# LayerNorm's factor rows, SiLU results and gated branch in PSUM instead of SBUF, and all low weights of that stage on GpSimd

## The chip, the cores and the metric

The kernel runs on one core of one Trainium2 chip. The metric is the device time of one execution in microseconds; smaller is better. The engines are TensorE (PE), VectorE (DVE), ScalarE (ACT), GpSimd (POOL) and the DMA queue of SyncE (SP). SBUF is the working memory, PSUM the eight banks that TensorE writes its products to.

## The reference, cut to what matters

Two layers on 512 tokens of width 1024, all in fp32. The change lies in the end of the first layer, between the convolution and the output projection.

```
u = a * sigmoid(b)                         # a, b, z = three parts of h @ w_in, 2048 channels each
c = depthwise causal convolution(u, 31 taps) + dw_b
mu, var = mean and variance of c over the 2048 channels of a token
cn = (c - mu) * rsqrt(var + EPS) * ln_g + ln_b
y  = silu(cn) * silu(z)
x  = x + y @ w_out                         # then layer 2: retention, and a last RMSNorm
```

## The kernel before, in words

Activations are held with channels in the partitions: the 2048 inner channels are 16 tiles of [128 channels, 512 tokens], one PSUM bank or 2 KB per partition each. Products in fp32 precision are made of three fp32r products: each operand is split into a high part (a rounded copy, by ScalarE) and a low part (the rest, a subtraction), and high x high, high x low and low x high are summed in PSUM. The same is done to the weights, which come as pairs of units of [128, 1024]: `whi(n)` is ScalarE's rounding of unit n (L181), `wlo(n, eng)` the subtraction by VectorE or GpSimd (L186). Of the raw weights two pairs fit into SBUF, of the high parts two pairs, of the low parts three.

The stage in question is LayerNorm and the output projection of layer 1 (L820 to L909). TensorE first sums over channels, VectorE makes the mean's rest `delta` and the factor `r` from [128, 4] values in 14 tiny operations (`rsqrt`, L249 to L261), and TensorE spreads each of the two over all partitions as a [128, 512] row in PSUM (`bcast_mm`, L267): `MUF` holds the mean, `RLp` the factor. ScalarE copies them to SBUF as `MU1` (L831) and `RL` (L894). While these small steps run, TensorE works off two gate units that were held back for it (`hold`, units 46 and 47).

Then, tile by tile (j = 0 to 15), `ln_a(j)` subtracts `MU1` (GpSimd, L859, five tiles ahead), `ln_b(j)` multiplies by the factor (VectorE, L863) and applies SiLU with gain and bias (ScalarE, L864), two tiles ahead; L884 multiplies by the gate `sz[j]` (VectorE), L886 rounds to the high part (ScalarE), L899 subtracts for the low part (VectorE), and twelve products of TensorE (L907 to L909, four output tiles of three) add the tile into four PSUM banks `acc4`. All of it stands in SBUF, except the rows `MUF` and `RLp` and the banks of `acc4`. Of the low weights, units 48, 50, 52, 54, 56 and 57 are GpSimd's and units 49, 51, 53 and 55 VectorE's.

In this stage every engine takes its instructions strictly in the order of the code. Behind it (L916 on) a scheduler orders them; the rotary tables (L935 to L967) are some 60 operations of VectorE that may begin behind the last `ln_b`, and the other half of the output projection (units 56 to 63, `x1_tile`) runs on TensorE meanwhile.

PSUM's eight banks are three pools: `MM` (5), `ACC` (2) and `ST` (1).

Of the kernel before, what the change touches and what calls it, by code (L numbers as in the profile page):

```python
# [20 lines left out]
S = 512            # tokens  # L21
NT = S // P        # token tiles
KD = 8             # 128-channel tiles of the model width
KI = 16            # 128-channel tiles of the inner width
W = 31             # taps
# [3 lines left out]
NU = 128           # weight units of [128, 1024]  # L29
PRODS = 3          # products that wait for GpSimd  # L30
ACCS = 2           # pairs of tiles with a sum of GpSimd
STEPS = 4          # at most so many taps of a pair of tiles are added by transfers
PAIRS = (2, 3, 4, 5)   # pairs of tiles with such taps
URING = 10         # tiles of the convolution's input
SPLIT = 12         # from this tile on VectorE and GpSimd have sums of their own (about M0)
APART = (1,) + tuple(range(SPLIT, KI))  # tiles with two sums
POOL_CAP = 16      # at most so many taps of a tile are summed by ScalarE and GpSimd
LEAD = 8           # taps that the last tile but one is ahead of the last
RATE = 1.6         # a product and its addition, as far as the choice of the next tile goes
MUP = 4            # so many of the first tiles TensorE sums for M0  # L40
HOLD = 2           # units that fill the gaps about the LayerNorm
GAP = 0.6          # products between two of its sums, so that TensorE's clock stays up
RESTS = 3          # sums of the last squares that are kept apart so
QLATE = 0.7        # margin for the end of the last transfer of squares
LNW = 2.8          # from the sums to the LayerNorm's factor
AHEAD = 5          # tiles that are centred ahead
TAILW = 10         # products that keep the clock up at the end
DMA_LAG = 1.55     # from the issue of a transfer to its start
# [6 lines left out]
def f12(v):  # L55
    """The nearest value with 12 significant bits."""
    m, e = np.frexp(v)
    return float(np.ldexp(np.round(m * 4096.0), int(e)) / 4096.0)
# [13 lines left out]
class Clock:  # L72
    """Estimated times (us) of engines that take instructions strictly in the order in which they are traced."""
# [13 lines left out]
    def land(self, cost, issued, key=None):  # L87
        """The end of a transfer."""
        return self.run(DMA_, cost, None, key, at=issued + DMA_LAG) + 0.1


@with_exitstack
def trunk(ctx: ExitStack, tc: tile.TileContext, xT, pos, wpack, conv_par, norms, freq, decay, out):
# [34 lines left out]
    def keep_warm(n):  # L128
        """Products of zeros: the tensor engine's clock drops to half when it idles."""
        o = ACC()  # L130
        for _ in range(n):
            nc.tensor.matmul(o, wz[:, 0:P], wz, start=True, stop=True)
# [56 lines left out]
    def neg_hi(p):  # L189
        """The high parts of a pair, negated, in the place of the low parts."""  # L190
        new_lo(p)
        it.run(ACT_, 1.8, lambda: nc.scalar.activation(los[p], raws[p], AF.Copy, scale=-1.0), f"wneg{p}")  # L192
# [5 lines left out]
    def dma_lo(p):  # L198
        """The transfer adds the weights to their negated high parts."""
# [18 lines left out]
    def split(src, eng=None, new=None):  # L218
        """src (fp32 in SBUF) as the exact sum of two fp32r tiles."""
# [5 lines left out]
    def mm3(o, a, b, first, last):  # L225
        """o += a.T @ b for split a and b."""
# [4 lines left out]
    def cm_proj(n, xs, k0=0, o=None, kt=KD, total=KD):  # L231
        """Channel-major projection of one unit (8 k-tiles x 128 columns)."""
# [8 lines left out]
    def rsqrt(v, scale=None, new=None):  # L241
        """v ** -0.5, or (v * scale + EPS) ** -0.5: a guess from the exponent's bits, a step of second order with
        constants that suit the guess's error, a step of third order."""
# [11 lines left out]
        # y is -guess / RSQRT_B; e = v guess ** 2; the result is guess (15 - 10 e + 3 e ** 2) / 8  # L255
# [8 lines left out]
    def bcast_mm(r4, o):  # L264
        """Per-token values [128 tokens, 4] as rows: [128, 512], the same in every partition."""
# [10 lines left out]
    def token_sums(tiles, o=None, first=True, last=True):  # L276
        """Sums over channels (partitions of all tiles), token-major [128, 4]."""
# [57 lines left out]
    # The taps of a tile: ScalarE multiplies and GpSimd adds the first ones, VectorE does the rest, on two tiles in  # L335
    # turn. How many are the first ones is set by how far GpSimd has come when VectorE gets to the tile. Some of the
    # products, of two tiles at once, are added by a transfer. The last tiles have a sum of VectorE, from the last tap
    # down, and one of GpSimd, from the first tap up.
    low = [0] * KI             # taps below are ScalarE's and GpSimd's
    high = [W] * KI            # in the last tiles: taps from here on are VectorE's  # L340
    acc_sb = [None] * KI       # GpSimd's sum
    acc_at = [0.0] * KI        # when it is there
    acc_ps = [None] * KI       # VectorE's sum
    begun = [0]                # tiles that VectorE has begun
    active = []
    latest = [None]            # the tile of VectorE's last instruction
    sums2 = {}                 # the places of GpSimd's sums, for two tiles each
    left2 = {}                 # how many of the two are not yet taken up
    freed = [0.0] * ACCS       # [n]: when the place of pair n is free
    steps = [0] * (KI // 2)    # taps of a pair of tiles that transfers add  # L350
    adds2 = deque()            # products of pairs that are yet to be added
    p2_free = [0.0]            # when their place is free
    adds = deque()             # products that GpSimd is yet to add
    stats = {"mu": 0, "d": 0, "pe": deque(), "sq": deque()}
    add_end = [0.0] * PRODS    # [n]: when the slot of product n is free
# [8 lines left out]
    def first_tap(j):  # L364
        """Tap 0 and the bias."""
# [12 lines left out]
    def release(j):  # L378
        """VectorE has taken up GpSimd's sum of tile j."""
# [4 lines left out]
    def room(j):  # L384
        """Whether tile j has a place for GpSimd's sum."""
        return j // 2 in sums2 or sum(n > 0 for n in left2.values()) < ACCS

    def pair_of(n):
        """The tiles of pair n that the next transfer can add to."""
# [67 lines left out]
    def ready(j):  # L457
        """When VectorE's next instruction of tile j can start."""
# [51 lines left out]
    def settled(j):  # L510
        """Whether the next product can be added to GpSimd's sum of tile j soon."""
        return acc_at[j] < it.now[POOL_] + 1.0 and all(a[0] != j // 2 for a in adds2)

    def pool_tile():
        """The tile that the next product is for."""
# [51 lines left out]
    # sums for LayerNorm: of the first tiles for M0, then of c - M0 (in the place of c) and of its square  # L567
# [696 lines left out]
```

## Time and profile before

| | |
|---|---|
| runs | 822.84, 824.01 and 825.59 us; median 824.01 us |
| profiled execution, first to last instruction | 821.5 us |
| TensorE busy in it | 790.3 us (96%) |
| VectorE, ScalarE, GpSimd busy | 606.6, 420.6 and 366.0 us |
| mean granted TensorE clock | 0.993 of 2.4 GHz |

For the profiled execution there is the span alone, 821.5 us; the runs, taken without the profiler, are 1.3 to 4.1 us longer than that, their median 2.5 us. The shares are means over stages with different limits; the stage of the change is some 60 us of the 821.5. Times within the trace count from the first instruction.

### The profile page before, as it was taken

What the parts mean: (1) busy time and instruction counts of PE and PEld (TensorE: products, weight loads), DVE (VectorE), ACT (ScalarE), POOL (GpSimd) and SP (SyncE); (2) the same over time, 40 slices, a digit from 0 to 9 for tenths busy, and PEclk for the clock granted to TensorE, in tenths of its full rate; (3) what the DMA queues carried; (4) which work ended last, traced back from release to release, by engine and by line L of the source; (5) the groups of instructions that cost most, each with busy time, mean ns of one, the idle gap of its engine ahead of it and who ended that gap; (6) DMA issues with size and microseconds to landing.
All of it is one profiled execution on the core that took longest, in us unless ns stands there. A gap on an engine that the chain in (4) does not pass through costs nothing.

```text
span 821.5 us, 9673 instructions
## 1 busy us (share of the span) xinstructions
PE 790.3 (96%) x3650; PEld 646.2 (79%) x3650; DVE 606.6 (74%) x852; ACT 420.6 (51%) x546; POOL 366.0 (45%) x287
## 2 busy tenths in 40 slices
PE   7889999999999998899999999999999999999996
PEld 3468878888888886578788888888888888888895
DVE  4788999999999979999955658566476557552324
ACT  4558888887987835444422433413423524341421
POOL 1439999999999975521311124223340122000300
PEclk9999999999999999999999999999999999999998
DMA  7497877887799742222232112213112212213103
GB/s 269 103 223 187 202 178 184 218 216 204 194 227 230 187 118 111 116 103 102 103 103 102 52 52 103 99 55 103 52 52 103 102 52 103 103 65 132 60 1 102
DMA packets 19901, 104.18 MB, mean 127 GB/s; under 512 B 2320, under 2 KB 5392, under 8 KB 8720
## 3 DMA queue, kind: packets, MB, share of 16 engines
q1 hardware_dynamic: 15392, 75.27, 25.7%
q0 software_dynamic: 4464, 28.31, 17.4%
q8 instruction: 28, 0.46, 0.2%
q14 instruction: 17, 0.14, 0.0%
HBM read 73.17 MB, written 2.10 MB: 92 GB/s over the span
## 4 chain that ended last, share of the span: by engine, by line
PE 78%; DVE 8%; POOL 4%; DMA 3%; ACT 3%; issue 3%; SPq 0%; DVEq 0%; POOLq 0%; ACTq 0%
PE mm L227 24%; PE mm L229 24%; PE mm L228 24%; DVE acc L497 3%; POOL accp L293 2%; DVE g L884 1%; DVE g L899 1%; DMA g<-xT 1%; DMA raw<-wpack 1%; POOL g L662 1%; ACT g L886 1%; DMA wlo<-raw 1%; PE dsum L282 1%; PE st L282 1%; DVE g L863 1%
## 5 line engine op out<-in xcount | busy, mean ns | idle before, releaser
L227 PE MATMUL mm<-g,whi 128*128 128x512 f32 (+1 forms) x832 | 320.2, 385 | 0.0
L229 PE MATMUL mm<-g,wlo 128*128 128x512 f32 (+1 forms) x832 | 316.9, 382 | 3.3 <-DMA wlo<-raw 3.3
L228 PE MATMUL mm<-g,whi 128*128 128x512 f32 (+1 forms) x832 | 317.4, 381 | 0.0
L497 DVE SCALAR_TENSOR_TENSOR acc<-u,cpar,acc 128x512 f32<-128x512 f32 x311 | 209.8, 746 | 0.5
L293 POOL TENSOR_TENSOR accp<-accp,prod 128x512 f32<-128x512 f32 x138 | 190.0, 1402 | 9.9 <-ACT prod L427 3.4
L229 PEld LDWEIGHTS mm<-g,wlo 128*128 128x128 f32 x832 | 156.5, 188 | 33.5 <-DMA wlo<-raw 3.7
L227 PEld LDWEIGHTS mm<-g,whi 128*128 128x128 f32 x832 | 156.5, 188 | 30.5 <-issue 1.2
L228 PEld LDWEIGHTS mm<-g,whi 128*128 128x128 f32 x832 | 156.5, 188 | 30.3 <-issue 1.2
L181 ACT CAST whi<-raw 128x1024 fp32r<-128x1024 f32 x80 | 80.5, 1048 | 101.3 <-PE mm L228 57.4
L186 DVE TENSOR_TENSOR wlo<-raw,whi 128x1024 fp32r<-128x1024 f32 x74 | 100.5, 1389 | 41.2 <-ACT whi L181 41.2
L293 POOL TENSOR_TENSOR g<-g,g 128x512 f32<-128x512 f32 x23 | 34.2, 1488 | 181.3 <-ACT g L289 172.7
L427 ACT ACTIVATE prod<-u,cpar 128x512 f32<-128x512 f32 x138 | 95.0, 717 | 25.7 <-POOL accp L293 25.2
L995 POOL TENSOR_TENSOR g<-g,g 128x512 f32<-128x512 f32 x8 | 10.3, 1293 | 140.0 <-DVE g L993 140.0
L222 DVE TENSOR_TENSOR g<-g,g 128x512 fp32r<-128x512 f32 x36 | 29.0, 820 | 35.7 <-ACT g L221 32.2
L221 ACT CAST g<-g 128x512 fp32r<-128x512 f32 x36 | 22.4, 621 | 60.0 <-POOL g L995 27.8
L228 PE MATMUL mm<-wlo,g 128*128 128x512 f32 x128 | 49.8, 389 | 0.0
L229 PE MATMUL mm<-whi,g 128*128 128x512 f32 x128 | 49.6, 389 | 0.0
L227 PE MATMUL mm<-whi,g 128*128 128x512 f32 x128 | 49.3, 389 | 0.0
L192 ACT ACTIVATE wlo<-raw 128x2048 fp32r<-128x2048 f32 x23 | 43.9, 1907 | 8.1 <-DMA raw<-wpack 8.1
L196 ACT CAST whi<-raw 128x2048 fp32r<-128x2048 f32 x23 | 43.7, 1898 | 0.0
L200 POOL DMA_DIRECT2D wlo<-raw x23 | 20.2, 877 | 38.1 <-ACT wlo L192 37.4
L1062 POOL TENSOR_TENSOR o<-o,g 128x512 f32<-128x512 f32 x16 | 27.5, 1749 | 18.2 <-DVE g L261 18.2
(193 smaller groups left out, 990.5 us busy)
## 6 DMA issues: line engine op xcount, KB each, us to landing
raw<-wpack SPq DMA_DIRECT2D x63, 1024.0 KB, 4.8
wlo<-raw POOLq DMA_DIRECT2D x23, 1024.0 KB, 7.2
g<-xT SPq DMA_DIRECT2D x16, 256.0 KB, 5.1
q<-q POOLq DMA_DIRECT2D x6, 512.0 KB, 7.5
out_dram<-xo SPq DMA_DIRECT2D x6, 256.0 KB, 2.3
dec<-decay SPq DMA_DIRECT2D x1, 1280.0 KB, 7.4
raw<-wpack SPq DMA_DIRECT2D x4, 256.0 KB, 5.9
accp<-prod POOLq DMA_DIRECT2D x2, 512.0 KB, 5.9
```

The lines of the kernel that those rows point to most:

```text
L181: it.run(ACT_, 0.95, lambda: nc.scalar.copy(his[p][:, i, :], raws[p][:, i, :]), f"whi{n}")
L186: it.run(e, c, lambda: eng.tensor_tensor(out=lo, in0=raws[n // 2][:, n % 2, :], in1=hi.bitcast(F32), op=ALU.subtract), f"wlo{n}", [f"whi{n}"])
L192: it.run(ACT_, 1.8, lambda: nc.scalar.activation(los[p], raws[p], AF.Copy, scale=-1.0), f"wneg{p}")
L196: it.run(ACT_, 1.8, lambda: nc.scalar.copy(his[p], raws[p]), f"whi{p}", deps)
L222: (eng or nc.vector).tensor_tensor(out=lo, in0=src, in1=hi.bitcast(F32), op=ALU.subtract)
L227: nc.tensor.matmul(o, a[0], b[0], start=first, stop=False)
L228: nc.tensor.matmul(o, a[0], b[1], start=False, stop=False)
L229: nc.tensor.matmul(o, a[1], b[0], start=False, stop=last)
L293: eng.tensor_tensor(out=a, in0=a, in1=b, op=ALU.add)
L427: at = it.run(ACT_, 0.61, lambda: nc.scalar.activation(p, u_sb[j][:, w:w + S], AF.Copy, scale=cpar[:, j, w:w + 1]), at=add_end[n_prod[0]])
L497: it.run(DVE_, cost, lambda: nc.vector.scalar_tensor_tensor(out=c_sb[j] if last else acc, in0=u_sb[j][:, w:w + S], scalar=cpar[:, j, w:w + 1],
L1062: nc.gpsimd.tensor_tensor(out=t, in0=t, in1=RO, op=ALU.mult)
```

## The change

The diff without its removed comments (line numbers of the code before are those of the kernel shown above):

```diff
@@ the bank that products of zeros go to, before the LayerNorm @@
-    idle = ACC()
+    idle = MM()
@@ LayerNorm's rows @@
     MUF = ACC()
     it.run(PE_, 0.86, lambda: bcast_mm(delta, MUF), "mu", at=t0 + 0.2)
     MU1 = G()
-    it.run(ACT_, 0.5, lambda: nc.scalar.copy(MU1, MUF), None, ["mu"])
     r = rsqrt(var)
-    wlo(49, nc.vector)
+    nc.vector.tensor_copy(MU1, MUF)
     work(t0 + LNW)
     RLp = ACC()
     it.run(PE_, 0.86, lambda: bcast_mm(r, RLp), "r", at=t0 + LNW)
-    RL = G()
@@ ln_a @@
-        nc.gpsimd.tensor_tensor(out=t, in0=t, in1=MU1, op=ALU.subtract)
+        if j < 2:
+            nc.vector.tensor_tensor(out=t, in0=t, in1=MUF, op=ALU.subtract)
+        else:
+            nc.gpsimd.tensor_tensor(out=t, in0=t, in1=MU1, op=ALU.subtract)
+    t_ps = {}
@@ ln_b @@
-        r = nc.vector.tensor_tensor(out=t, in0=t, in1=RLp if j < 3 else RL, op=ALU.mult)
-        nc.scalar.activation(t, t, AF.Silu, scale=cpar[:, j, W + 1:W + 2], bias=cpar[:, j, W + 2:W + 3])
+        r = nc.vector.tensor_tensor(out=t, in0=t, in1=RLp, op=ALU.mult)
+        t_ps[j] = t if j == 2 else (ACC, ST, MM)[j % 3]()
+        nc.scalar.activation(t_ps[j], t, AF.Silu, scale=cpar[:, j, W + 1:W + 2], bias=cpar[:, j, W + 2:W + 3])
@@ ahead of the loop, behind ln_a of five and ln_b of two tiles @@
+    wlo(49, nc.gpsimd)
@@ in the loop over j @@
-        t = c_sb[j]
+        t = t_ps.pop(j)
         nc.vector.tensor_tensor(out=t, in0=t, in1=sz[j], op=ALU.mult)
         hi, lo = G(F32R), G(F32R)
         nc.scalar.copy(hi, t)
-        if j % 4 == 2 and n > 49:
+        if j % 2 == 0 and n > 49:
             wlo(n + 1, nc.gpsimd)
...
-            nc.scalar.copy(RL, RLp)
...
         nc.vector.tensor_tensor(out=lo, in0=t, in1=hi.bitcast(F32), op=ALU.subtract)
-        if j % 4 == 0 and n > 49:
-            wlo(n + 1, nc.vector)
```

So `RLp` stays in PSUM for all 16 tiles, SiLU writes a PSUM bank (tile 2 alone stays in SBUF), the gate's product is made in that bank in place, and the rounding and the low part read it there. `MUF` is read by VectorE for tiles 0 and 1; the copy `MU1` is VectorE's, behind `rsqrt`. Units 49 to 57 of the low weights are all GpSimd's.

VectorE around the start of the stage, before (L261 ends `rsqrt`; `acc` is `RLp`, `g` are SBUF tiles):

```order
L260 TENSOR_TENSOR rs_2577<-rs_2577,rs_2576 128x4
L261 SCALAR_TENSOR_TENSOR rs_2575<-rs_2577,rs_2575 128x4
L186 TENSOR_TENSOR wlo_2489<-raw_2261,whi_2488 128x1024
L863 TENSOR_TENSOR g_290<-g_290,acc_2598 128x512
L863 TENSOR_TENSOR g_392<-g_392,acc_2598 128x512
L884 TENSOR_TENSOR g_290<-g_290,g_1804 128x512
L863 TENSOR_TENSOR g_640<-g_640,acc_2598 128x512
L899 TENSOR_TENSOR g_2674<-g_290,g_2673 128x512
L884 TENSOR_TENSOR g_392<-g_392,g_1856 128x512
L863 TENSOR_TENSOR g_657<-g_657,g_2603 128x512
```

The same place of the changed program (`acc_2568` is `MUF`, `acc_2597` is `RLp`, `acc_2641` and `st_2644` are the banks of tiles 0 and 1):

```order
L260 TENSOR_TENSOR rs_2576<-rs_2576,rs_2575 128x4
L261 SCALAR_TENSOR_TENSOR rs_2574<-rs_2576,rs_2574 128x4
L833 COPY g_2573<-acc_2568 128x512
L861 TENSOR_TENSOR g_290<-g_290,acc_2568 128x512
L861 TENSOR_TENSOR g_392<-g_392,acc_2568 128x512
L869 TENSOR_TENSOR g_290<-g_290,acc_2597 128x512
L869 TENSOR_TENSOR g_392<-g_392,acc_2597 128x512
L893 TENSOR_TENSOR acc_2641<-acc_2641,g_1804 128x512
L869 TENSOR_TENSOR g_640<-g_640,acc_2597 128x512
L907 TENSOR_TENSOR g_2675<-acc_2641,g_2674 128x512
L893 TENSOR_TENSOR st_2644<-st_2644,g_1856 128x512
```

The low weights of unit 49 have left VectorE and a copy and two subtractions of [128, 512] have come; from there on each operation of VectorE reads one tile from SBUF and one from PSUM, where before it read two from SBUF (tile 2 excepted).

GpSimd in the same stage, before (L859 is `ln_a`):

```order
L859 TENSOR_TENSOR g_900<-g_900,g_2573 128x512
L859 TENSOR_TENSOR g_1013<-g_1013,g_2573 128x512
L186 TENSOR_TENSOR wlo_2685<-raw_2378,whi_2684 128x1024
L859 TENSOR_TENSOR g_1106<-g_1106,g_2573 128x512
L859 TENSOR_TENSOR g_1298<-g_1298,g_2573 128x512
L859 TENSOR_TENSOR g_1439<-g_1439,g_2573 128x512
L859 TENSOR_TENSOR g_1541<-g_1541,g_2573 128x512
L859 TENSOR_TENSOR g_1699<-g_1699,g_2573 128x512
L186 TENSOR_TENSOR wlo_2794<-raw_2670,whi_2793 128x1024
```

And now (L863 is `ln_a`):

```order
L863 TENSOR_TENSOR g_900<-g_900,g_2573 128x512
L186 TENSOR_TENSOR wlo_2489<-raw_2261,whi_2488 128x1024
L863 TENSOR_TENSOR g_1013<-g_1013,g_2573 128x512
L186 TENSOR_TENSOR wlo_2685<-raw_2378,whi_2684 128x1024
L863 TENSOR_TENSOR g_1106<-g_1106,g_2573 128x512
L863 TENSOR_TENSOR g_1298<-g_1298,g_2573 128x512
L863 TENSOR_TENSOR g_1439<-g_1439,g_2573 128x512
L186 TENSOR_TENSOR wlo_2685<-raw_2378,whi_2684 128x1024
L863 TENSOR_TENSOR g_1541<-g_1541,g_2573 128x512
```

Units 49 and 51 stand between the tiles' subtractions now, and so do units 53 and 55 further on; tiles 0 and 1 are gone from here.

## Rows read from the trace of the kernel before

**Rows 1.** The page: span, busy time and share of each engine, instructions.

```profile
span 821.5 us, 9673 instructions
PE 790.3 (96%) x3650; PEld 646.2 (79%) x3650; DVE 606.6 (74%) x852; ACT 420.6 (51%) x546; POOL 366.0 (45%) x287
```

**Rows 2.** Stretches: length, busy (instructions) of PE PEld DVE ACT POOL, clock, DMA, GB/s.

```profile
296.40:306.67 10.27, 9.07 (x50) 7.29 (x49) 9.08 (x18) 4.02 (x7) 8.43 (x6) 1.00 0.43 134
306.67:363.76 57.09, 49.44 (x198) 36.81 (x198) 54.26 (x52) 27.87 (x40) 30.30 (x16) 0.97 0.29 105
363.76:406.50 42.74, 42.74 (x190) 35.42 (x189) 42.02 (x63) 17.23 (x25) 7.40 (x5) 1.00 0.28 99
```

**Rows 3.** Waits from 296.4 to 364 us: us in total, times, longest.

```profile
PE mm L909 <- DVE g L899: 7.7, 6, 2.0
```

**Rows 4.** TensorE in order of time: start, us, instruction [idle before].

```profile
300.82 1.16 PE L267 MATMUL acc<-ident,rs 128*128 128x128 f32 x8 [1.20 <-DVE rs L261]
...
306.67 0.58 PE L907 MATMUL mm<-g,whi 128*128 128x512 f32 x1
...
318.90 0.63 PE L907 MATMUL mm<-g,whi 128*128 128x512 f32 x1
...
363.76 0.39 PE L228 MATMUL mm<-g,whi 128*128 128x512 f32 x1
...
409.60 1.05 PE L282 MATMUL st<-ones,g 128*128 128x1 f32 x8 [1.02 <-POOL g L293]
```

**Rows 5.** VectorE in order of time, from the LayerNorm's factor on.

```profile
298.37 1.18 DVE L260 TENSOR_TENSOR rs<-rs,rs 128x4 f32<-128x4 f32 x1
299.58 1.19 DVE L261 SCALAR_TENSOR_TENSOR rs<-rs,rs 128x4 f32<-128x4 f32 x1
...
304.79 0.68 DVE L863 TENSOR_TENSOR g<-g,acc 128x512 f32<-128x512 f32 x1
...
309.26 2.45 DVE L899 TENSOR_TENSOR g<-g,g 128x512 fp32r<-128x512 f32 x1 [0.39 <-ACT g L886]
311.63 1.77 DVE L884 TENSOR_TENSOR g<-g,g 128x512 f32<-128x512 f32 x1
...
323.11 1.22 DVE L186 TENSOR_TENSOR wlo<-raw,whi 128x1024 fp32r<-128x1024 f32 x1
324.25 0.69 DVE L884 TENSOR_TENSOR g<-g,g 128x512 f32<-128x512 f32 x1
```

**Rows 6.** GpSimd in order of time; the first two rows begin at one instruction.

```profile
298.24 9.47 POOL L859 TENSOR_TENSOR g<-g,g 128x512 f32<-128x512 f32 x6 [4.89 <-ACT g L831]
298.24 2.51 POOL L859 TENSOR_TENSOR g<-g,g 128x512 f32<-128x512 f32 x2 [4.89 <-ACT g L831]
...
308.79 2.37 POOL L186 TENSOR_TENSOR wlo<-raw,whi 128x1024 fp32r<-128x1024 f32 x1 [1.07 <-ACT whi L181]
311.11 8.50 POOL L859 TENSOR_TENSOR g<-g,g 128x512 f32<-128x512 f32 x5
```

**Rows 7.** VectorE and GpSimd at the end of the convolution.

```profile
284.86 2.72 DVE L497 SCALAR_TENSOR_TENSOR acc<-u,cpar,acc 128x512 f32<-128x512 f32 x4
...
285.32 5.68 POOL L293 TENSOR_TENSOR accp<-accp,prod 128x512 f32<-128x512 f32 x4
```

**Rows 8.** ScalarE and VectorE by operation, 297 to 362 us: count | busy, mean ns.

```profile
L884 DVE TENSOR_TENSOR g<-g,g 128x512 f32<-128x512 f32 x16 | 18.0, 1124 | 0.3 <-ACT g L864 0.3
L864 ACT ACTIVATE g<-g,cpar 128x512 f32<-128x512 f32 x16 | 12.9, 815 | 7.7 <-DVE g L863 7.7
...
L886 ACT CAST g<-g 128x512 fp32r<-128x512 f32 x16 | 9.9, 621 | 23.2 <-DVE g L884 23.2
L181 ACT CAST whi<-raw 128x1024 fp32r<-128x1024 f32 x8 | 8.3, 1038 | 0.0
```

**Rows 9.** VectorE: first rotary operation, and the sum of output tile 6.

```profile
353.23 0.42 DVE L937 CAST o<-posi 128x512 f32<-128x512 int32 x1
...
400.29 0.68 DVE L922 TENSOR_TENSOR g<-g,mm 128x512 f32<-128x512 f32 x1
```

## The prediction

> **What bounds the kernel now.** The page comes first: TensorE is busy for 790.3 of 821.5 us [rows 1], so a change elsewhere can only give back what TensorE loses, and the question is how much of the missing 31 us lies in this stage. The stretches tell it: from 363.76 to 406.50 us TensorE is busy all the time and runs 190 products in 42.74 us [rows 2], one per 0.227 us (the two cut by the edges counted for half). From 306.67 to 363.76 us the projection's 192 products and four of the next one take 57.09 us [rows 2, 4], where 196 x 0.227 = 44.5 us would do. So 12.6 us are lost there. The view of the waits names most of it: TensorE waited 7.7 us, in six pieces, for L899, VectorE's low part of a tile [rows 3]; some products at 318 to 321 us run at the lower of the clock's two levels (one takes 0.63 us; the stretch's granted clock is 0.97) [rows 2, 4], about 1.5 us, and the rest is draining and restarting around each wait. Ahead of it TensorE waited 1.2 us for the factor from L261 [rows 4], and behind it, at 409.60 us, 1.02 us for sums that were late because VectorE was [rows 4].
>
> Why VectorE is late is seen by laying it beside GpSimd. In the stretch VectorE is busy for 54.26 of 57.09 us [rows 2]. The same L884 takes 0.69 us at 324.25, when GpSimd is idle, and 1.77 us at 311.63, during five `ln_a` of GpSimd in a row [rows 5, 6]; L899 takes 2.45 us when it begins inside a 2.37 us low weight of GpSimd [rows 5, 6]; even two operations on [128, 4] in `rsqrt` take 1.18 and 1.19 us once GpSimd has started at 298.24 [rows 5, 6]. All of these read two tiles from SBUF (L260 and L261 too). L863 at 304.79 reads one from SBUF and one from PSUM: it takes 0.68 us amid six `ln_a` of GpSimd, 298.24 to 307.71 [rows 5, 6], and L497, with one large SBUF operand and PSUM for the other and the result, needs 0.68 us each in the middle of GpSimd's additions [rows 7]. So it is the second SBUF operand that waits for GpSimd, and the change takes it away.
>
> **The change part by part.** *Start.* Before, GpSimd starts when ScalarE's copy `MU1` is done and so falls on the last two operations of `rsqrt`. Now the copy is behind `rsqrt` on VectorE, and GpSimd is idle until then: the two take 0.17 instead of 1.18 and 1.19 us (their twelve fellows' pace), 2.0 us less. TensorE can use only what it waited, and the products ahead of the factor's row end sooner by that: the row starts at about 299.46 instead of 300.82 us, and so does everything of TensorE behind it, **1.36 us**. On VectorE follow the copy and two subtractions from `MUF`, three operations of 0.68 us [rows 5], 298.8 to 300.8 us; the row is ready at 299.46 + 1.16 [rows 4] and a handoff, 300.7. So they are hidden by TensorE making the row; without that cover they would cost 2 us. Tile 0 then: factor until 301.4, SiLU 0.82, gate 0.69, rounding 0.62 [rows 8], low part, some 0.1 us between engines: ready at 304.4, and TensorE arrives at 305.3. Covered.
>
> *First tiles.* ScalarE rounds tile 1 behind two gate evictions and `whi(50)`. The second eviction waits for TensorE's last held product at 305.4, then 0.6 + 1.04 + 0.62 us (the eviction taken as a rounding) [rows 8]: 307.6, low part at 308.3; TensorE wants it at 308.5. Tile 2 stays in SBUF, and GpSimd is on unit 50 from 307 to 309.4: gate product at the end of that, 310.0, rounding 310.7, low part behind one `ln_a`, 311.9 to 312.4; TensorE wants it at 311.2. That is a remaining stall of 0.7 to 1.2 us; I take **1.0**.
>
> *Steady state, per tile.* TensorE 12 x 0.227 = 2.73 us. VectorE three operations of 0.69, with the rounding between, about 2.2 us in a chain. ScalarE 0.82 + 0.62 and half a `whi` of 1.04: 1.96 us [rows 8]. VectorE and ScalarE run ahead of TensorE by half a microsecond per tile. The three PSUM banks for SiLU are no new wait: tile j + 3's SiLU needs its factor product, which stands behind tile j's low part on VectorE anyway. So the 12.6 us go, but for the stall of 1.0.
>
> *Operands in PSUM.* Their price shows for factor rows (0.68) and in-place sums (0.68) [rows 5, 7], against 0.69 from SBUF [rows 5]: nothing. For a bound I let it be 0.05 us either way, 48 x 0.05 = 2.4 us of VectorE, which lies in its spare 0.5 us per tile. ScalarE writing a bank has no row here; I take its SBUF time, with 0.2 us either way (a quarter of 0.815), 3 us of ScalarE over the stage, covered too. The Trainium skill's page "VectorE: DVE Perf Modes", Rules for kernel authors, advises to copy a PSUM operand to SBUF first if many operations read it, which speaks against leaving the factor in PSUM for 16 tiles; its cycle table makes a PSUM read some 65 ns dearer, by which the sum would stay and VectorE's spare shrink by 3 us. The trace disagrees on the price, 0.68 from PSUM against 0.69 from SBUF [rows 5].
>
> *Low weights.* Units 49, 51, 53 and 55 cost VectorE 1.22 us each and now GpSimd 2.37 [rows 5, 6], with 14 `ln_a` of 1.25 (2.51 for two) left there: 14 x 1.25 + 9 x 2.37 = 38.8 us from 299.4 on. Unit 55 is needed for tile 14, at 305.3 + 1.0 + 14 x 2.73 = 344.5; up to it GpSimd has 34.1 us of work, so 11 us of slack, and between 4 and 5 if each `ln_a` took its crowded 1.70 (8.50 for five). Behind each waits a load of raw weights (two pairs fit), as before behind VectorE's; unit 51 ends at about 318, its successor's load has 10 us until it is wanted.
>
> *Behind the stage.* VectorE reaches the last `ln_b`, and with it the rotary tables, at about 339 us instead of 353.23, that is 14 us earlier; what TensorE gains until then is 13. So the sum of output tile 6, at 400.29 [rows 9] and thus 4.7 us behind TensorE's end of that tile (363.76 and 140 products, 395.6), comes about on time, and the 1.02 us at 409.60 go: **1.0**. Layer 2 keeps its order.
>
> *Sum.* 1.36 + (12.6 - 1.0) + 1.0 = 13.9 us. I take off 0.4 for small waits at tile ends and get 821.5 - 13.5 = 808.0 us of span; with the 2.5 us by which the median run exceeds the profiled span, **810.5 us**.
>
> **The rivals.** *GpSimd becomes the bound.* For it: elementwise work of GpSimd takes 1.94 times VectorE's (2.37 to 1.22), in-order waits for `whi` can stop the `ln_a` queued behind a low weight, and VectorE waits for these. Against: the 11 us of slack. If the crowded times hold and each of the four moved units delays the tiles by 1 to 2 us, 4 to 8 us come back: 814.5 to 818.5 us. The Trainium skill's page "GPSIMD Engine Reference", section on elementwise cycle accounting, holds two-input elementwise work to be VectorE's because GpSimd takes about twice as long; the trace agrees on the ratio.
>
> *The gain is given back behind the stage*: VectorE is busy for 42.02 of 42.74 us there [rows 2], and if the rotary tables still end at 396 us rather than 382, TensorE waits for output tiles 3 to 6 in the next projection; 10 us of the 13.9 return: 820.
>
> *The change doesn't do what it says.* If VectorE's operations wait for GpSimd whatever their operand, only 3.7 us of moved low weights and the 2 us of `rsqrt` remain, spent on three new operations: 822 to 825, no change. Rows 5 and 7 speak against it.
>
> *Slower.* An operation that reads and writes one bank in place, on a bank that ScalarE just wrote, takes two passes, 1.4 us: with 3 operations of 1.4 a tile takes 4.2 us on VectorE, 16 x 4.2 = 67 us instead of 57, 834 us. It decides from 57.09 / 48 = 1.19 us per operation on. L497 at 0.68 [rows 7] does the same in place.
>
> **How the numbers follow.** No change is within 0.3%, about 2.5 us, the least that a measurement of this kernel can tell. Forecast (808.5 to 813) 0.62; better still (no stall at tile 2, or gains in layer 2) 0.08; GpSimd 0.18; given back 0.05; no effect 0.03; slower 0.04. Faster is the first four: 0.93. The range 807 to 817 leaves out slower, no effect, given back and the end of GpSimd's case.
>
> **What would show it.** Right: L893 and L907 at 0.7 us all through, also beside GpSimd; L260 and L261 at 0.17 us; the factor's row at 299.5 us; one wait of TensorE for a low part, at tile 2, and 12 products per 2.73 us; no lower clock; the projection's last product near 351 us. Wrong: waits of TensorE for L186 on GpSimd or of VectorE for L863, SiLU or L893 above 1 us, or TensorE idle between 351 and 397 us.

## The result, and the profile after

The changed kernel takes 808.86 us (median of 4 runs, 807.0 to 811.59) against 824.8 us for the kernel before in the same comparison (its three runs of the table above and one of 826.37 us): a ratio of 0.9823, with a 95% interval of 0.9803 to 0.9842. It is faster by 16 us. The forecast was 810.5 us in a range of 807 to 817.

The page of the changed kernel's profiled execution answers to [rows 1]: span, then busy time and share of each engine.

```profile
span 805.4 us, 9669 instructions
PE 785.6 (98%) x3648; PEld 647.1 (80%) x3650; DVE 582.7 (72%) x851; ACT 418.9 (52%) x544; POOL 368.6 (46%) x289
```

The span has lost 16.1 us. TensorE's idle time has fallen from 31.2 to 19.8 us, and it is 4.7 us less busy as well. VectorE is 24 us less busy. Some 3 us of that is work that has moved (four low weights of 1.22 us gone, three operations of 0.68 us come); the rest is the same work in less time.

TensorE in order of time: start, duration, and in brackets the idle time ahead with what ended it.

```profile
294.99 1.14 PE L267 MATMUL acc<-ident,delta 128*128 128x128 f32 x8
...
298.05 1.05 PE L267 MATMUL acc<-ident,rs 128*128 128x128 f32 x8
...
303.79 0.58 PE L913 MATMUL mm<-g,whi 128*128 128x512 f32 x1
...
310.26 0.50 PE L915 MATMUL mm<-g,whi 128*128 128x512 f32 x1 [0.19 <-DVE g L907]
...
349.15 0.39 PE L915 MATMUL mm<-g,whi 128*128 128x512 f32 x1
...
393.13 0.95 PE L282 MATMUL st<-ones,g 128*128 128x1 f32 x8
```

The second row is that of the factor: no wait ahead of it where 1.20 us stood [rows 4]. The fourth is the only listed wait for a low part in the whole projection. The last, the token sums behind the projection, waited 1.02 us before [rows 4] and waits no more. Stretches of that time, with the same columns as [rows 2]:

```profile
303.79:349.15 45.36, 45.17 (x198) 37.06 (x199) 38.09 (x59) 26.54 (x38) 34.28 (x20) 1.00 0.43 159
349.15:393.13 43.98, 43.98 (x196) 36.41 (x195) 40.23 (x56) 18.93 (x26) 11.67 (x6) 1.00 0.27 96
```

TensorE is busy for all but 0.19 of 45.36 us, at the full clock, while VectorE has 7 us to spare. VectorE by operation from 297 to 350 us (count | busy, mean ns | idle before): `acc`, `st` and `mm` are PSUM banks.

```profile
L869 DVE TENSOR_TENSOR g<-g,acc 128x512 f32<-128x512 f32 x16 | 10.7, 677 | 0.0
...
L893 DVE TENSOR_TENSOR acc<-acc,g 128x512 f32<-128x512 f32 x6 | 4.1, 690 | 0.3 <-ACT acc L872 0.3
L907 DVE TENSOR_TENSOR g<-acc,g 128x512 fp32r<-128x512 f32 x6 | 4.1, 690 | 1.0 <-ACT g L895 0.6
```

The gate's product, 1.124 us on the mean before [rows 8], now takes 0.69 us, and no operation of this stretch with a PSUM operand takes more than 0.70 us, beside GpSimd or alone. Tile 2, left in SBUF, is the check within the same run; VectorE in order of time:

```profile
296.96 0.16 DVE L260 TENSOR_TENSOR rs<-rs,rs 128x4 f32<-128x4 f32 x1
297.15 0.16 DVE L261 SCALAR_TENSOR_TENSOR rs<-rs,rs 128x4 f32<-128x4 f32 x1
...
306.60 1.90 DVE L893 TENSOR_TENSOR g<-g,g 128x512 f32<-128x512 f32 x1
...
309.19 1.01 DVE L907 TENSOR_TENSOR g<-g,g 128x512 fp32r<-128x512 f32 x1
```

Its two operations take 1.90 and 1.01 us amid neighbours of 0.69. GpSimd itself, 297 to 350 us:

```profile
L186 POOL TENSOR_TENSOR wlo<-raw,whi 128x1024 fp32r<-128x1024 f32 x9 | 21.8, 2419 | 6.4 <-ACT whi L181 6.3
L863 POOL TENSOR_TENSOR g<-g,g 128x512 f32<-128x512 f32 x14 | 18.7, 1356 | 6.1 <-DVE g L833 6.1
```

**Where the 16.1 us of span come from.** From marks in both traces, before against after:

- The row of the mean's difference starts at 296.40 and at 294.99 us: 1.41 us that lie ahead of everything the change touches. They are lost and won at the start of the program, where nothing is changed, by eight products that took 5.38 us before and 3.68 after, at another clock (from 17 to 20 us the granted clock is 0.63 before and 1.00 after). I put them down to chance: over all profiles of this document that row starts anywhere from 294.22 to 297.92 us.
- From there to the factor's row: 4.42 and 3.06 us, 1.36 us.
- To the projection's first product: 5.85 and 5.74 us, 0.11 us.
- From the first product to the token sums behind the projection: 306.67 to 409.60 is 102.93 us, 303.79 to 393.13 is 89.34 us, 13.59 us.
- From the sums to the end: 411.90 and 412.27 us, a loss of 0.37 us.

The products of the first point, before and then after:

```profile
16.88 5.38 PE L322 MATMUL mm<-g,raw 128*128 128x512 f32 x8
```

```profile
17.13 3.68 PE L322 MATMUL mm<-g,raw 128*128 128x512 f32 x8
```

The stretch of the fourth point leaves out the chance at the start, so the experiments below are compared by it ("the stage") beside the time.

### The profile page after: what moved, and what is told of

It reads as the page before. It is cut to its first block, busy times and chain, and to the rows that moved or that the text cites. A ratio compares the mean times of both kernels' runs of the same rounds, so it can differ in the third digit from the quotient of the medians.

```text
span 805.4 us, 9669 instructions
## 1 busy us (share of the span) xinstructions
PE 785.6 (98%) x3648; PEld 647.1 (80%) x3650; DVE 582.7 (72%) x851; ACT 418.9 (52%) x544; POOL 368.6 (46%) x289
## 4 chain that ended last, share of the span: by engine, by line
PE 93%; DMA 3%; DVE 1%; issue 1%; POOL 1%; ACT 1%; SPq 0%; DVEq 0%; ACTq 0%; POOLq 0%
PE mm L227 28%; PE mm L229 27%; PE mm L228 27%; DMA g<-xT 2%; PE mm L915 2%; PE mm L913 2%; PE mm L914 2%; POOL g L662 1%; DMA wlo<-raw 1%; PE dsum L282 1%; PE st L282 1%; PE acc L229 1%; PE acc L228 1%; PE acc L227 1%; PE st L623 0%
## 5 line engine op out<-in xcount | busy, mean ns | idle before, releaser
L186 DVE TENSOR_TENSOR wlo<-raw,whi 128x1024 fp32r<-128x1024 f32 x70 | 94.4, 1383 | 41.1 <-ACT whi L181 41.1
```

The lines of the kernel that those rows point to most:

```text
L186: it.run(e, c, lambda: eng.tensor_tensor(out=lo, in0=raws[n // 2][:, n % 2, :], in1=hi.bitcast(F32), op=ALU.subtract), f"wlo{n}", [f"whi{n}"])
```

## The experiments

All medians are of 4 runs unless said otherwise; the kernel before took 823.68, 823.96 and 824.05 us (7 to 13 runs) in the three comparisons. All profiles together:

```
kernel                                      first product  sums     stage    time, us  ratio to before [95%]
before                                      306.67         409.60   102.93   823.7 to 824.8
low weights moved, nothing else             304.58         413.48   108.90   828.23    1.0059 [1.0041, 1.0077]
factor rows in PSUM + low weights moved     306.67         409.98   103.31   823.70    1.0003 [0.9991, 1.0016]
factor rows in PSUM                         305.50         405.03    99.53   819.25    0.9941 [0.9924, 0.9958]
gate's result in PSUM too + low w. moved    305.86         403.98    98.12   817.50    0.9930 [0.9908, 0.9953]
gate's result in PSUM too                   304.27         398.59    94.32   812.27    0.9860 [0.9846, 0.9875]
all in PSUM, low weights as before          306.86         396.66    89.80   809.17    0.9821 [0.9800, 0.9843]
all in PSUM + low weights moved (after)     303.79         393.13    89.34   808.86    0.9823 [0.9803, 0.9842]
the same, second comparison                 304.62         393.97    89.35   809.27    0.9824 [0.9803, 0.9845]
SiLU and branch in PSUM, factor in SBUF     307.81         403.87    96.06   816.57    0.9911 [0.9889, 0.9933]
the same, rotary tables behind              304.75         396.83    92.08   811.34    0.9854 [0.9834, 0.9874]
before without GpSimd's subtractions        306.49         398.79    92.30   812.86    0.9861 [0.9827, 0.9895]
after, the mean's copy on ScalarE           308.18         397.60    89.42   810.19    0.9838 [0.9816, 0.9859]
before, that copy on VectorE                306.07         409.59   103.52   822.89    0.9995 [0.9981, 1.0008]
```

Each stage is that of one profile, and falls of TensorE's clock inside it are part of it: the mean granted clock of the stage is 0.98 in the kernel before and in the run with SiLU and branch in PSUM and the factor in SBUF; it is 0.97 with the low weights moved alone, with the gate's result in PSUM and low weights moved, and in the last row; in all others it is 1.00. By length and clock that costs an estimated 2 us in the first two and 3 us in the other three.

**Low weights alone.** The kernel before, with units 49, 51, 53 and 55 moved to GpSimd.

```diff
@@ behind rsqrt @@
-    wlo(49, nc.vector)
@@ behind ln_b of two tiles @@
+    wlo(49, nc.gpsimd)
@@ in the loop over j @@
-        if j % 4 == 2 and n > 49:
+        if j % 2 == 0 and n > 49:
             wlo(n + 1, nc.gpsimd)
...
-        if j % 4 == 0 and n > 49:
-            wlo(n + 1, nc.vector)
```

> The kernel before, with the low weights of units 49, 51, 53 and 55 moved from VectorE to GpSimd and nothing else. Theory (VectorE's operations with two SBUF operands wait for GpSimd): VectorE loses 4.9 us of its own work but meets four more GpSimd operations of 2.4 us, each of which holds one of its operations for 1 to 2 us more; no gain, 822 to 829 us, and TensorE's waits for L899 stay at 6 us or more. Rival (VectorE simply had too much work, and the moved 4.9 us are the gain): 817 to 820 us, waits for L899 down to 3 us.

Measured 828.23 us, 4.5 us slower than before in its comparison (823.68). Its waits of TensorE, and VectorE by operation, before and then in this run, show why:

```profile
PE mm L907 <- DVE g L899: 12.9, 10, 3.1
```

```profile
L899 DVE TENSOR_TENSOR g<-g,g 128x512 fp32r<-128x512 f32 x16 | 20.5, 1280 | 3.0 <-ACT g L886 2.6
...
L863 DVE TENSOR_TENSOR g<-g,g 128x512 f32<-128x512 f32 x13 | 12.1, 934 | 0.0
```

```profile
L899 DVE TENSOR_TENSOR g<-g,g 128x512 fp32r<-128x512 f32 x16 | 22.3, 1392 | 2.7 <-ACT g L886 2.3
...
L862 DVE TENSOR_TENSOR g<-g,g 128x512 f32<-128x512 f32 x13 | 15.4, 1185 | 0.0
```

VectorE is rid of four operations of 1.22 us, 4.9 us in all, and loses more than that: its low parts go from 1.28 to 1.39 us on the mean, its factor products from tile 3 on from 0.93 to 1.19 us, and over the stage it is busy for 103.6 us instead of 99.4. A low part that begins inside a GpSimd low weight lasts until some 0.5 us behind that one's end, so up to 2.47 us. TensorE's waits grow from 7.7 [rows 3] to 12.9 us.

**The PSUM moves alone.** The changed kernel, with the low weights back on VectorE as before (the diff above in reverse).

> The changed kernel with the low weights of units 49, 51, 53 and 55 back on VectorE. Theory: PSUM operands are what counts and VectorE has some 0.5 us per tile to spare, so four operations of 1.2 to 2.4 us cost at most 2 us: 808.5 to 812 us. Rival (the moved low weights carry the gain): 814 us or more.

Measured 809.17 us, the same as the full change. So the moved low weights are worth nothing where VectorE is no longer late, and the gain is that of the other edits: the operands, and with them the start and the two subtractions that went from GpSimd to VectorE.

**Factor rows only.** The changed kernel with SiLU and branch in SBUF: one of VectorE's three operations per tile reads PSUM (in the kernel before, the factor's product did so for tiles 0 to 2 alone).

```diff
-        t_ps[j] = t if j == 2 else (ACC, ST, MM)[j % 3]()
+        t_ps[j] = t
```

> The changed kernel with SiLU's result and the gated branch in SBUF again; the two factor rows stay in PSUM, the low weights on GpSimd. Theory: the gate's product and the low part read two SBUF tiles again and take 1.7 us beside GpSimd, the factor's product 0.68: the start's 1.4 us and a third of the rest, 815 to 822 us. Rival (the row in PSUM and the start are the gain): 808 to 811 us.

Measured 823.70 us (10 runs): no gain, outside what was expected. VectorE by operation:

```profile
L907 DVE TENSOR_TENSOR g<-g,g 128x512 fp32r<-128x512 f32 x16 | 22.8, 1422 | 3.0 <-ACT g L895 1.7
L893 DVE TENSOR_TENSOR g<-g,g 128x512 f32<-128x512 f32 x16 | 19.1, 1197 | 0.3 <-ACT g L872 0.3
L869 DVE TENSOR_TENSOR g<-g,acc 128x512 f32<-128x512 f32 x16 | 10.7, 677 | 1.6 <-PE acc L267 1.6
```

The factor product falls to 0.68 us, as it should; the two that still read two SBUF tiles are as long as with the low weights moved alone. Whether the rows are worth nothing or their gain was eaten was left to this run:

**Factor rows, low weights as before.**

> Factor rows in PSUM as in the run with the rows alone, low weights as before the change. If the moved low weights ate the rows' gain (moved alone they cost 4.5 us of time, and from the projection's first product to the sums behind it 108.9 us instead of 102.9), that stretch falls from 103.3 to 97-99 us and the time is 817-820 us. If one PSUM operand in three is worth nothing by itself, the stretch stays above 101.5 us and the time is 821.5-825 us.

Measured 819.25 us, with a stage of 99.53 us, half a microsecond above the first case's range and well below the second's. The rows, with the two subtractions that GpSimd is rid of, are worth 3.4 us of the stage, and the moved low weights 3.8 us the other way. No run tells the rows from those two subtractions.

**SiLU in SBUF, the gate's product into PSUM.** Only the place of SiLU's result differs from the changed kernel, and with it one operand of L893.

```diff
-        nc.scalar.activation(t_ps[j], t, AF.Silu, ...
+        nc.scalar.activation(t, t, AF.Silu, ...
...
-        nc.vector.tensor_tensor(out=t, in0=t, in1=sz[j], op=ALU.mult)
+        nc.vector.tensor_tensor(out=t, in0=c_sb[j], in1=sz[j], op=ALU.mult)
```

> The changed kernel with SiLU's result in SBUF: the gate's product then reads two SBUF tiles and writes the PSUM bank, the rounding and the low part read the bank as in the changed kernel. Theory (it is the second SBUF input that waits, wherever the result goes): the gate's product takes up to 1.8 us beside GpSimd, the low part 0.69; VectorE's spare of 8 us takes most of it, 808.5 to 814 us. Rival (the place of the result counts): the gate's product at 0.7 us all through.

Measured 817.50 us, slower than expected. Its VectorE:

```profile
L893 DVE TENSOR_TENSOR acc<-g,g 128x512 f32<-128x512 f32 x6 | 8.7, 1448 | 0.3 <-ACT g L872 0.3
...
L907 DVE TENSOR_TENSOR g<-acc,g 128x512 fp32r<-128x512 f32 x6 | 4.1, 690 | 0.7 <-ACT g L895 0.3
```

A result in PSUM doesn't help an operation that reads two SBUF tiles: 1.45 us, against 0.69 when one of them is in PSUM. It is the inputs that count. The expectation held VectorE's spare to be enough for it; it isn't, since 0.68 + 1.45 + 0.69 = 2.82 us per tile exceed TensorE's 2.73. Over 16 tiles that is only 1.4 us of the 8.8 by which the stage is longer than the changed kernel's. More stands at the end; VectorE and TensorE in order of time, and a stretch with the columns of [rows 2]:

```profile
347.49 2.72 DVE L959 SCALAR_TENSOR_TENSOR o<-o,o 128x512 f32<-128x512 f32 x1
```

```profile
350.87 0.80 PE L915 MATMUL mm<-g,whi 128*128 128x512 f32 x1 [2.39 <-DVE g L907]
```

```profile
350.87:360.00 9.13, 9.13 (x27) 7.24 (x28) 8.93 (x14) 1.53 (x2) 2.37 (x1) 0.67 0.32 117
```

L959 belongs to the rotary tables. It reads two SBUF tiles and began inside a GpSimd low weight (347.29 to 349.66 us); the low part behind it was late, TensorE waited 2.39 us and then ran at a mean clock of 0.67 for 9.13 us, which costs 3.0 us.

**The same, low weights as before.**

> SiLU in SBUF, gate's product into PSUM, factor rows in PSUM, low weights as before the change. If a low weight on GpSimd costs VectorE's gate product (two SBUF operands) its 1.2 us of waiting, the stretch from the projection's first product to the sums falls from 98.1 to 93-96 us: 812.5-815.5 us. If GpSimd's subtractions alone crowd it as much, or VectorE's own 1.22 us per low weight takes the gain back: 97-99 us, 816-819 us.

Measured 812.27 us, with a stage of 94.32 us: 3.8 us better than with the low weights moved, the first case (the time 0.2 us below its range). The clock did not fall in this stage, and TensorE waited 0.3 us for a low part instead of 2.7.

**Branch only.** The changed kernel with the factor copied to SBUF (`RL`) from tile 3 on, as before the change.

```diff
+    RL = G()
...
-        r = nc.vector.tensor_tensor(out=t, in0=t, in1=RLp, op=ALU.mult)
+        r = nc.vector.tensor_tensor(out=t, in0=t, in1=RLp if j < 3 else RL, op=ALU.mult)
...
         if j == 0:
+            nc.scalar.copy(RL, RLp)
```

> The changed kernel with the factor row copied to SBUF by ScalarE again from tile 3 on; SiLU and the gated branch in PSUM. Theory: the factor's product alone reads two SBUF tiles and takes up to 1.7 us, 16 times at most 1.1 us more, against VectorE's spare 8 us over the stage: 809 to 815 us, with the 0.69 us of the gate's product and the low part unchanged. Rival (nothing but the branch counts): the same as the changed kernel within 1 us.

Measured 816.57 us, outside the range. The factor product (L870) is crowded, 1.28 us on the mean, which leaves VectorE at 2.66 us per tile: enough on the mean. TensorE waited only twice for a low part, 1.86 us at tile 2 and 2.38 us at the end; VectorE, GpSimd and TensorE there, in order of time:

```profile
348.68 2.72 DVE L961 SCALAR_TENSOR_TENSOR o<-o,o 128x512 f32<-128x512 f32 x1
351.32 0.68 DVE L909 TENSOR_TENSOR g<-mm,g 128x512 fp32r<-128x512 f32 x1
```

```profile
348.48 2.37 POOL L186 TENSOR_TENSOR wlo<-raw,whi 128x1024 fp32r<-128x1024 f32 x1 [4.16 <-ACT whi L181]
```

```profile
352.05 0.50 PE L917 MATMUL mm<-g,whi 128*128 128x512 f32 x1 [2.38 <-DVE g L909]
352.39 0.54 PE L915 MATMUL mm<-g,whi 128*128 128x512 f32 x1
352.73 0.63 PE L916 MATMUL mm<-g,wlo 128*128 128x512 f32 x1
```

The end is that of the run with SiLU in SBUF again. The rotary tables may begin behind the last factor product, so the scheduler put some of them ahead of the low parts of tiles 14 and 15. L961 reads two SBUF tiles and met a GpSimd low weight, so it took 2.72 instead of 0.69 us; the low part behind it came late; TensorE waited 2.38 us and then ran products at the lower clock, 0.63 us for one instead of 0.39. The stretch from 352.05 to 359.89 us has a granted clock of 0.78, which is half clock for 44% of 7.84 us and costs 1.7 us. In the changed kernel VectorE is far enough ahead for the same order to do no harm (tables from 334.05 us on).

**The same, rotary tables behind the last low part.**

```diff
-        nc.vector.tensor_tensor(out=lo, in0=t, in1=hi.bitcast(F32), op=ALU.subtract)
+        last_ln = nc.vector.tensor_tensor(out=lo, in0=t, in1=hi.bitcast(F32), op=ALU.subtract)
```

> Branch and SiLU in PSUM with the factor in SBUF, as in the run with the branch only, but the rotary tables stand behind the last tile's low part instead of behind the last factor product. If the end of that run was lost because the tables (one of 2.72 us beside a low weight of GpSimd) stood ahead of the last two low parts, its wait of 2.4 us and the some 3 us of products at the lower clock behind it go: from the first product to the sums 90.5-92.5 us instead of 96.1, 810.5-813.5 us. If the tables, now 10 us later, hold up the sums behind the projection, or the waits only move to earlier tiles: 95-97 us, 815-818 us.

Measured 811.34 us, with a stage of 92.08 us, the first case: the order at the end cost 4.0 us of the 6.7 by which that kernel's stage is longer than the changed kernel's. What remains is one wait of 1.9 us at tile 2 and 0.4 us behind the projection.

**No centring.** The kernel before, with GpSimd's 16 subtractions of the mean left out (that part of the computation is missing). Nothing of it is in PSUM that wasn't before.

> The kernel before without GpSimd's 16 subtractions of the mean (left out: the mean's rest is not subtracted). All operands stay in SBUF, the low weights as before. Theory (contention with GpSimd): VectorE's operations take 0.69 us outside GpSimd's five low weights, rsqrt's last two 0.17: 9 to 13 us faster than before, 812 to 816 us. Rival (SBUF operands are slow by themselves or PSUM is the faster place): VectorE's operations stay at a mean above 0.9 us, and the time within 2 us of before.

```profile
L883 DVE TENSOR_TENSOR g<-g,g 128x512 f32<-128x512 f32 x16 | 10.9, 684 | 0.3 <-ACT g L863 0.3
L862 DVE TENSOR_TENSOR g<-g,g 128x512 f32<-128x512 f32 x13 | 8.9, 684 | 0.0
...
L898 DVE TENSOR_TENSOR g<-g,g 128x512 fp32r<-128x512 f32 x16 | 18.2, 1138 | 4.9 <-ACT g L885 4.0
```

Measured 812.86 us. The SBUF pairs of L883 and L862 take 0.684 us, all of them, once GpSimd's subtractions are gone. Of GpSimd's work in the stage the low weights remain, and four low parts of VectorE (L898) begin inside one; the first, and the GpSimd instruction that it meets:

```profile
308.73 2.46 DVE L898 TENSOR_TENSOR g<-g,g 128x512 fp32r<-128x512 f32 x1 [1.98 <-ACT g L885]
```

```profile
308.26 2.37 POOL L186 TENSOR_TENSOR wlo<-raw,whi 128x1024 fp32r<-128x1024 f32 x1 [15.20 <-ACT whi L181]
```

These four take 2.46 to 2.49 us and the other twelve 0.68 or 0.69: one instruction, one kind of operand, and only the neighbour differs. So nothing is slow about two SBUF operands as such; it takes GpSimd at work beside them.

**The start: the mean's copy on ScalarE.** The changed kernel with `MU1` copied by ScalarE ahead of `rsqrt`, so that GpSimd starts early, as before.

```diff
+    it.run(ACT_, 0.5, lambda: nc.scalar.copy(MU1, MUF), None, ["mu"])
     r = rsqrt(var)
-    nc.vector.tensor_copy(MU1, MUF)
```

> The changed kernel with the mean's copy on ScalarE ahead of rsqrt, as in the kernel before, so that GpSimd starts during rsqrt. Theory: the last two operations of rsqrt take 1.2 us again, the factor's row is 1.2 to 1.4 us later against the mean's, and so is the first product of the projection: 1.0 to 1.5 us slower than the changed kernel. Rival (rsqrt's slowness has another cause, or the later row is hidden): rsqrt at 0.17 us, or the projection not later.

```profile
299.89 1.17 DVE L260 TENSOR_TENSOR rs<-rs,rs 128x4 f32<-128x4 f32 x1
301.10 1.19 DVE L261 SCALAR_TENSOR_TENSOR rs<-rs,rs 128x4 f32<-128x4 f32 x1
```

```profile
PE acc L267 <- DVE rs L261: 1.2, 1, 1.2
```

The two operations on [128, 4] take 1.17 and 1.19 us again and TensorE waits 1.2 us again. The factor's row starts 4.42 us behind the row of the mean's difference, as before. The time is 810.19 us (ratio 0.9838, 0.9816 to 0.9859), some 1 us above the changed kernel's, within the intervals: the cause of the wait is shown, its price in time is not.

**The start alone.** The kernel before with the copy on VectorE behind `rsqrt`.

> The kernel before with the mean's copy on VectorE behind rsqrt and nothing else. Theory: rsqrt's last two operations at 0.17 us, the factor's row and the projection's first product 1.0 to 1.4 us earlier, GpSimd's first subtraction 1.2 us later, no effect on the stalls behind: 1 us faster, 822 to 825 us, seen in the trace rather than in the times. Rival (the later GpSimd delays tiles 3 on): the end of the projection not earlier.

Measured 822.89 us (10 runs; 0.9995, 0.9981 to 1.0008): a gain of this size can't be told from none. In its trace L260 and L261 take 0.16 us and the wait is gone, and yet the factor's row starts 4.65 us behind the row of the mean's difference, against 4.42 before, so the expected earlier row did not come. The clock fell there; the window from 296 us on (the clock is the last but two):

```profile
296.00:298.00 2.00, 2.00 (x10) 1.90 (x9) 1.66 (x12) 0.00 (x0) 0.00 (x0) 0.50 0.00 0
```

**The changed kernel once more.** Nothing altered; the question was that clock.

> The changed kernel, nothing altered. If TensorE's lower clock behind the statistics (at 296-300 us in six profiles, not in the first one of this kernel) comes by chance of the execution, this profile may show it too, and then the factor's row starts 4.6 instead of 3.06 us behind the row of the mean's difference and the span is 1.5 us longer for it; from the first product to the sums 89.3 us either way. Time 807-811 us. If it belongs to the kernels that were altered: no lower clock there, 3.06 us again.

Measured 809.27 us. This execution shows the lower clock too; the windows of the two executions of one program, this one first:

```profile
295.00:297.20 2.20, 2.20 (x9) 2.00 (x9) 1.96 (x10) 0.00 (x0) 0.00 (x0) 0.50 0.00 0
```

```profile
295.00:297.20 2.20, 2.20 (x16) 1.99 (x16) 1.69 (x11) 0.00 (x0) 0.00 (x0) 1.00 0.00 0
```

TensorE is busy in both and gets 9 instructions done against 16, so the factor's row starts 4.66 us behind the other row instead of 3.06. The stage is 89.35 us, as in the first execution to 0.01 us.

## Why the prediction was right

**The mechanism** held: an operation of VectorE that reads two SBUF tiles waits for a GpSimd instruction that runs beside it, and one that reads a tile from PSUM doesn't. Three kernels show it from three sides: one operand moved away (0.69 us for 1.12), GpSimd's subtractions removed (0.684, and 2.46 to 2.49 where a low weight still runs beside it), the result alone moved (1.45). The rival "doesn't do what it says" fell with them, and so did "slower" by two passes in place: L893 in place takes 0.69 us.

**The start, 1.36 us,** measured 1.36 in the profiled execution, and that is luck. The cause held: L260 and L261 take 0.16 or 0.17 us and the wait is gone in all 11 profiles in which GpSimd starts behind `rsqrt` or not at all. But the term is paid only when the products ahead of the factor's row run at the full clock, and in 9 of these 11 they did not: in the second profile of the changed kernel the row comes 4.66 us after the other, 0.24 later than it did while waiting. The prediction counted on the full clock here. In the time the term is not told from nothing.

**The projection, 12.6 us lost, 11.6 back.** After, 197 products start in the 45.36 us up to the projection's last (191 of it and six of the next one; the row's 198 has one that began ahead of it); at 0.227 us each they need 44.7, so some 0.6 is lost and 12.0 came back. The step that was mis-sized is the remaining stall at tile 2, taken as 1.0 us: it measured 0.19. The gate's product took 1.90 us, as crowded as foreseen, but the low part behind it only 1.01: with the 1.41 us of the start added, it was ready at 311.6 us where 311.9 to 312.4 was foreseen, and TensorE wanted it at 311.3 where 311.2 was.

**Behind the stage, 1.0 us:** the 1.02 us went, and about 0.6 us of small gaps with it. The rotary tables began at 334.05 us (339 was foreseen, 1.4 of it chance), and nothing waited behind them, so "given back behind the stage" fell.

**The sum.** 1.36 + 0.11 + 13.59 - 0.37 = 14.7 us of span are the change's in the first profile, where 13.5 were foreseen; 1.4 more are the luck of that profile. In the second, with the lower clock at the start, the change's share is 821.5 - 806.3 - 2.2 = 13.0 us (2.2 being what that execution gained ahead of the change). The two medians, of four runs each, lie 1.6 and 1.2 us below the forecast's 810.5.

**PSUM's price.** 0.677 us (L869) and 0.69 us (L893, L907) with a PSUM operand against 0.684 from SBUF with GpSimd out of the way: nothing. The Trainium skill's page "VectorE: DVE Perf Modes", Rules for kernel authors, leaves the choice between reading a matmul's output in PSUM and copying it to SBUF first where many operations follow. Here the copy costs time: the run with the branch only makes it for the factor, and its stage is 6.7 us longer, 2.7 us with the rotary tables behind.

**Low weights.** The prediction gave them a slack of 11 us on GpSimd and held them harmless. In the changed kernel they are: 21.8 + 18.7 = 40.5 us of work where 38.8 were foreseen, and TensorE never waits for them. But it did not say that they bring nothing (89.80 against 89.34 us), nor that their price hangs on the other edits: 6.0, 3.8 and 3.8 us of the stage, and 4.5, 4.8 and 5.3 us of the median time, while VectorE has three, two or one operation per tile with two SBUF operands. The rival's 4 to 8 us were the right size for those kernels, by another way: not GpSimd being late, but VectorE held up by it.

**What an edit is worth hangs on the others.** With the low weights left alone, the factor rows give 3.4 us, the gate's result in PSUM with its low part 5.2 more, SiLU's result in PSUM 4.5 more; taken out of the full change, the factor row alone costs 6.7. The expectation for the rows missed because it gave the moved low weights no price: with them back it was met. Those for the branch and for SiLU in SBUF missed because they took VectorE's mean per tile against TensorE's; rotary tables in front of the last tiles made one tile late, and then came the lower clock (with the factor in SBUF tile 2 was late as well, 1.86 us).

## What to carry to other kernels

When two engines are at work on SBUF, look for the same instruction's time with and without the other's neighbour before you count instructions: VectorE's 0.69 us had become 0.9 to 1.3 us on the mean and up to 2.5 us here, and one input in a PSUM bank was the cure. Moving work from the late engine to the idle one can cost more than it relieves when the idle engine's work is what holds up the late one (4.9 us moved, 6.0 us lost). Judge a stage by two marks inside the trace beside the median time, since what lies ahead of the change moved single profiles by up to 3.7 us here; and look at the clock between the marks, since its falls are in the stage too, some 2 to 3 us in five of the 14 profiles.

## What the runs showed of the hardware that was not expected

- ScalarE is faster at PSUM: SiLU into a bank takes 0.78 us against 0.815 into SBUF [rows 8], and rounding from a bank 0.58 against 0.621 [rows 8]; tile 2, in SBUF in the changed kernel too, takes 0.82 and 0.62 there. The changed kernel's ScalarE by operation, 297 to 350 us:

```profile
L872 ACT ACTIVATE acc<-g,cpar 128x512 f32<-128x512 f32 x6 | 4.7, 786 | 6.7 <-DVE g L869 6.7
...
L895 ACT CAST g<-acc 128x512 fp32r<-128x512 f32 x6 | 3.5, 583 | 3.2 <-DVE acc L893 3.1
```

- The wait goes both ways. GpSimd's 16 subtractions took 26.5 us before, 1.69 us on the mean (five in a row 8.50 us [rows 6]). In the changed kernel two of them beside VectorE's PSUM operands take 1.26 us each:

```profile
325.45 2.52 POOL L863 TENSOR_TENSOR g<-g,g 128x512 f32<-128x512 f32 x2
```

- The wait for GpSimd is not by size: an operation on 4 elements per partition goes from 0.16 to 1.18 us.
- TensorE's clock fell to the lower level, 1.2 GHz, between 294 and 298 us in 9 of the 11 profiles in which GpSimd didn't crowd `rsqrt`, with TensorE busy all along, behind a stretch in which single-column sums and [128, 128] rows stand between its products, and rose some 3 us later. It fell in none of the three in which `rsqrt` was crowded, although it falls ahead of the place where the crowding begins. Whether that is more than chance stays open.
